# Convolution module of a hybrid decoder step: tap seeds in PSUM, thirds of a tile in strict order, sums of squares of two norms added up by TensorE

## The chip, the cores and the metric

The kernel runs on one core of one Trainium2 chip. The metric is the device time of one execution in microseconds, the median of the runs taken.

## The reference

One step of a two-layer decoder with D = 1024, for a prompt of 1024 tokens behind 16 meta tokens and for 8 sequences with 4 new tokens each. Layer 0 is a Conformer convolution module and a ConvFFN; layer 1 is attention over a latent paged cache and another ConvFFN. Everything is float32. The change touches the convolution module alone:

```python
def conv_module(x, prefix, w_pw1, b_pw1, w_dw, b_dw, ln_g, ln_b, w_pw2, b_pw2):
    a, g = jnp.split(x @ w_pw1 + b_pw1, 2, axis=-1)       # x is rms_norm(h): 1024 -> 2 x 1024
    u = a * jax.nn.sigmoid(g)
    y, tail = causal_dwconv(u, prefix, w_dw)              # 31 taps for each channel
    y = jax.nn.silu(layer_norm(y + b_dw, ln_g, ln_b))
    return y @ w_pw2 + b_pw2, tail                        # 1024 -> 1024

def key_nope(c, w_uk, knorm_nope):                        # c: a page of the cached latent, 128 x 128
    return rms_norm(jnp.einsum('btc,chd->bthd', c, w_uk), knorm_nope)
```

`key_nope` of the cache is needed late, in layer 1; its sums of squares depend on the cache alone, so the kernel uses that product as a filler from the start on.

## The kernel before

Activations lie transposed: 8 tiles of 128 channels (KD = 8) by T0 = 1074 columns of tokens, with NB = 9 blocks of 128 tokens. A float32 product is made of three passes (`xh`, `xl`: high and low part of the data; `wh`, `wl`: of the weights). A **filler** (`cache_norms`) is one group of work on the cache: three matmuls of 512 columns (L603) and the sum of squares of 8 heads of 64, in one of three ways: 8 ACT squares with an accumulator (L615); one ACT square (L606) and a DVE reduction (L611); or the square, two halvings on POOL (L610) and a short DVE reduction. `on_dve` and `on_pool` say which of the eight groups of a page set goes which way, and `HALVE` where POOL stops. There are 256 groups. `self.help` sends the splits of the cache pages (`cl`) to POOL instead of DVE.

The module runs in these stages:

- **First norm** (from L347). For each of 8 tiles ACT squares it (L275, L278) and DVE adds the square to a sum (L279); nine ones-matmuls (L287, 18 records of one pass each) turn the sum into one number per token, DVE makes 1/sqrt of it in 11 small operations (`rsqrt`, L251 to L256), and `spread` brings it to all partitions: a copy on DVE (L264), transposes (L266), a copy on ACT (L268). Then the tiles are scaled (L354) and split (L135 ACT, L136 DVE). 30 fillers are put into this stage (`FIRST`).
- **Tile 0** of the first product (`gemms`, 144 matmuls of 358 columns, L171), without fillers of its own.
- **Tiles 1 to 7** of the first product: a tile is cut into three thirds of 358 columns, each with a value and a gate half (48 matmuls, L395), a filler after every 6 matmuls. Behind a third come the sigmoid (L378, ACT) and the product u (L379, DVE). Each half has two PSUM banks. The scheduler, which sees the whole program, may let thirds overlap.
- **conv31**, for each tile, beside the next tile's product: DVE does 46 multiply-adds of 512 columns (L488): 16 taps for even, 15 for odd positions (`p0`, `p1`) and 16 for a combined sequence `s` = u odd + u even shifted (L477, `p2`). The running sum (`a0`, `a1`) lies in PSUM. The first term of each comes from ACT (L481) and is written to SBUF, into `fa` or `fb`. POOL makes the products for the last columns (L484) and for the 8 sequences (L502), which DVE reduces (L486, L504).
- **layer_norm**: the mean by TensorE (L529, 3 matmuls for each of 8 tiles, fillers between them: `FILL1` 2, `FILL0` 11), centering (L537, DVE), squares (L543, ACT), their sum on DVE and POOL (L549, L546, L551), then ones-matmuls, rsqrt and spread as above, with 15 fillers (`FILL2`) and 4 more behind (`NLN`).
- **pw2**: scaling (L426), SiLU (L428), split, and the second product (L171), with a filler after every 9 matmuls as long as there are any.

`high_priority` raises an operation for the scheduler; `manual_schedule` fixes TensorE's order as written, and `follow` adds an order without a wait.

Of the kernel before, what the change touches and what calls it, by code (L numbers as in the profile page):

```python
# [25 lines left out]
NB = 9  # L26
# [9 lines left out]
FILL0 = 11  # L36
FILL1 = 2
FILL2 = 15
NLN = 4
ONDVE0 = ()  # L40
ONDVE = (0,)
ONLN = (0, 4)
# [76 lines left out]
class Prog:  # L119
# [139 lines left out]
    def spread(self, r9, out, tn, ps=None):  # L259
# [3 lines left out]
        for c in range(3):  # L263
            nc.vector.tensor_copy(rx[:, 3 * c:3 * c + 3], r9[:, 3 * c:3 * c + 3].rearrange("p (a b) -> p a b", b=1).broadcast_to([128, 3, 128]))  # L264
            for b in range(3):
                nc.tensor.transpose(ps[:, c, b * 128:(b + 1) * 128], rx[:, 3 * c + b, :], self.cst("ident"))  # L266
            w = min(384, tn - 384 * c)
            nc.scalar.activation(out[:, 384 * c:384 * c + w], ps[:, c, :w], AF.Copy)  # L268

    def sq_add(self, sq, x, k, tn):  # L270
        nc = self.nc
        if k == 0:
            if sq.shape[1] > T0:
                nc.gpsimd.memset(sq[:, tn:], 0.0)
            nc.scalar.activation(sq[:, :tn], x, AF.Square)  # L275
            return
# [14 lines left out]
    def rows_rstd(self, sq, tn):  # L291
        r9, ps = self.token_rstd(self.sp, [sq[:, 128 * b:128 * (b + 1)] for b in range(NB)])
# [28 lines left out]
    def conv_phase(self):  # L321
# [3 lines left out]
        with ExitStack() as es:  # L325
# [40 lines left out]
            for c in range(KD):  # L366
                self.help = 0 < c < KD - 1
# [19 lines left out]
                else:  # L387
                    ch, cnt = T0 // 3, 0
                    for t in range(3):
                        ps = [p.tile([128, 1, 512], F32, name="g")[:, :, :ch] for p in (ga, gg)]  # L390
                        with self.manual():
                            for w, p in zip(ws, ps):
                                for k in range(KD):
                                    for i, (x, m) in enumerate(((w[0], xh), (w[0], xl), (w[1], xh))):
                                        nc.tensor.matmul(p[:, 0], x[:, k * 128:(k + 1) * 128], m[k][:, t * ch:t * ch + ch],  # L395
                                                         start=k == 0 and i == 0, stop=k == KD - 1 and i == 2)
# [3 lines left out]
                        glu(*ps, t)  # L400
                with self.manual():
# [30 lines left out]
            self.on_dve, self.on_pool = ONLN, ONPL1  # L432
# [3 lines left out]
            sq = self.rp.tile([128, T0], F32, name="sq")  # L436
            ahead = [self.weight(a["pw2"][ot], 1024) for ot in range(2)]
# [32 lines left out]
    def conv31(self, c, u, us, y, w31, wsum, pr):  # L470
# [6 lines left out]
        nc.vector.tensor_tensor(out=s, in0=u[:, 1, 0:535], in1=u[:, 0, 1:536], op=ALU.add)  # L477
        def taps(p, x, w, n, name):
# [5 lines left out]
            nc.gpsimd.tensor_tensor(out=r, in0=bass.AP(v.tensor, v.offset, [list(v.ap[0]), [1, m - ND], [1, n]]),  # L484
                                    in1=w.rearrange("p (c j) -> p c j", c=1).broadcast_to([128, m - ND, n]), op=ALU.mult)
# [16 lines left out]
        nc.gpsimd.tensor_tensor(out=p, in0=win, in1=w31[:, c:c + 1].broadcast_to([128, NS, 31]), op=ALU.mult)  # L502
# [16 lines left out]
    def layer_norm(self, ys):  # L519
# [4 lines left out]
        self.on_dve = ONLN0  # L524
        self.on_pool = ONPL0
# [5 lines left out]
        self.on_dve = ONLN  # L531
        self.on_pool = ONPL1
        sq = self.tp.tile([128, 1152], F32, name="sq", tag="c")
        odd = None
        with self.tc.high_priority(PRIO):
            for k in range(KD):
                nc.vector.scalar_tensor_tensor(out=v3(ys[k]), in0=mu[:, :, :ch], scalar=-1.0 / D, in1=v3(ys[k]), op0=ALU.mult, op1=ALU.add)  # L537
            for k in range(KD):
                if k == 0:
                    self.sq_add(sq, ys[k], 0, T0)  # L540
                    continue
                q = self.xpool(k).tile([128, self.tw], F32R, name=f"xl{k}").bitcast(F32)
                nc.scalar.activation(q, ys[k], AF.Square)  # L543
                if k in ONPOOL:
                    if odd is not None:
                        nc.gpsimd.tensor_tensor(out=odd, in0=q, in1=odd, op=ALU.add)  # L546
                    odd = q if odd is None else odd
                else:
                    nc.vector.tensor_tensor(out=sq[:, :T0], in0=sq[:, :T0], in1=q, op=ALU.add)  # L549
                if k == ADDAT:  # L550
                    nc.vector.tensor_tensor(out=sq[:, :T0], in0=sq[:, :T0], in1=odd, op=ALU.add)  # L551
# [15 lines left out]
    def cache_open(self, es):  # L567
# [12 lines left out]
        self.fill = self.cache_norms()  # L580
        self.on_pool = ()

    def cache_norms(self):
# [10 lines left out]
        for g in range(32):  # L594
            ch, cl = nxt
            for j in range(4):
                p = 4 * g + j
                for c in range(2):
# [1238 lines left out]
```

## Time and profile before

| | us |
|---|---|
| median of 3 runs (lowest to highest) | 2837.03 (2835.17 to 2849.47) |
| the profiled execution | 2836.05 |
| its span in the profile | 2834.3 |

| engine | busy us | share of the span |
|---|---|---|
| TensorE (PE) | 2675.1 | 94% |
| VectorE (DVE) | 1911.5 | 67% |
| ScalarE (ACT) | 1380.9 | 49% |
| GpSimd (POOL) | 665.5 | 23% |

The mean granted TensorE clock was 0.966 of full speed. Times in the rows below are microseconds from the start of the span. TensorE's matmuls are pipelined: the distance between two starts is what one costs, its own duration is longer.

### The profile page before, as it was taken

What the parts mean: (1) busy time and instruction counts of PE and PEld (TensorE: products, weight loads), DVE (VectorE), ACT (ScalarE), POOL (GpSimd) and SP (SyncE); (2) the same over time, 40 slices, a digit from 0 to 9 for tenths busy, and PEclk for the clock granted to TensorE, in tenths of its full rate; (3) what the DMA queues carried; (4) which work ended last, traced back from release to release, by engine and by line L of the source; (5) the groups of instructions that cost most, each with busy time, mean ns of one, the idle gap of its engine ahead of it and who ended that gap; (6) DMA issues with size and microseconds to landing.
All of it is one profiled execution on the core that took longest, in us unless ns stands there. A gap on an engine that the chain in (4) does not pass through costs nothing.

```text
span 2834.3 us, 47489 instructions
## 1 busy us (share of the span) xinstructions
PE 2675.1 (94%) x16916; PEld 2456.8 (87%) x16916; DVE 1911.5 (67%) x3521; ACT 1380.9 (49%) x4074; POOL 665.5 (23%) x923
## 2 busy tenths in 40 slices
PE   7999986999999999999799999988999999999999
PEld 5888864999999999999667676656999999999999
DVE  8899997569888874234776767565358777766131
ACT  6778778435554553023555564555335544544010
POOL 1457542005333330001201212100005333321000
PEclk9999997999999999999889999978999999999999
DMA  4111110412322236122100001257502222227122
GB/s 136 55 39 57 40 48 20 153 47 76 101 80 91 85 115 225 40 93 90 37 10 26 23 16 42 73 168 225 183 33 76 72 86 78 79 86 257 45 85 74
DMA packets 127778, 238.30 MB, mean 84 GB/s; under 512 B 39779, under 2 KB 81141, under 8 KB 127413
## 3 DMA queue, kind: packets, MB, share of 16 engines
q1 hardware_dynamic: 103828, 200.82, 22.1%
q0 software_dynamic: 9600, 32.36, 3.1%
q10 hardware_dynamic: 14112, 2.09, 0.4%
q8 instruction: 133, 2.18, 0.3%
q14 instruction: 105, 0.85, 0.1%
HBM read 183.90 MB, written 51.31 MB: 83 GB/s over the span
## 4 chain that ended last, share of the span: by engine, by line
PE 80%; DVE 7%; ACT 6%; DMA 2%; issue 2%; SPq 2%; POOL 0%; ACTq 0%; DVEq 0%
PE ps L742 29%; PE ps L171 22%; PE v L1280 5%; PE pk L603 4%; PE ps L791 3%; PE g L395 3%; PE p L147 2%; DVE a L488 2%; PE ps L193 2%; ACT qq L615 2%; PE ps L960 1%; PE p L1290 1%; PE s L1250 1%; PE p L1292 1%; PE p L1293 1%
## 5 line engine op out<-in xcount | busy, mean ns | idle before, releaser
L135 ACT ACTIVATE wh<-raw 128x512 fp32r<-128x512 f32 (+2 forms) x256 | 191.3, 750 | 566.3 <-PE ps L171 360.0
L136 DVE TENSOR_TENSOR wl<-raw,wh 128x512 fp32r<-128x512 f32 (+2 forms) x244 | 201.1, 828 | 104.9 <-ACT wh L135 102.8
L888 DVE TENSOR_TENSOR x<-ps,x 128x1074 f32<-128x1074 f32 (+1 forms) x48 | 60.9, 1270 | 289.5 <-PE ps L171 289.4
L712 DVE SCALAR_TENSOR_TENSOR c<-ub,c,c 128x1040 f32<-128x1040 f32 (+1 forms) x176 | 225.2, 1312 | 30.1 <-ACT c L709 29.3
L615 ACT ACTIVATE qq<-pk 128x64 f32<-128x64 f32 x936 | 198.2, 248 | 76.8 <-PE pk L603 76.2
L615 ACT ACTIVATION_READ_ACCUMULATOR qq<-pk 128x1 f32 x936 | 194.3, 232 | 0.1
L1280 PE MATMUL v<-pf,vf 128*128 128x512 f32 (+4 forms) x448 | 180.2, 486 | 11.8 <-ACT pf L1297 11.5
L707 POOL COPY sb<-ub 128x32 f32<-128x32 f32 x88 | 88.4, 1006 | 398.1 <-DVE ub L753 359.6
L610 POOL TENSOR_TENSOR sq<-sq 128x256 f32<-128x256 f32 x198 | 130.1, 659 | 181.7 <-ACT sq L606 174.4
L603 PE MATMUL pk<-ukh,ch 128*128 128x512 f32 x256 | 115.2, 451 | 47.2 <-ACT qq L615 17.1
L1297 ACT ACTIVATE pf<-p 128x512 f32<-128x512 f32 (+4 forms) x224 | 99.5, 450 | 122.9 <-DVE p L1295 102.2
L171 PE MATMUL ps<-xh,wh 128*128 128x358 f32 (+1 forms) x672 | 147.8, 328 | 2.6 <-DVE x L888 1.6
L171 PE MATMUL ps<-xh,wl 128*128 128x358 f32 (+1 forms) x672 | 147.3, 327 | 0.4 <-DVE wl L136 0.4
L171 PE MATMUL ps<-al,wh 128*128 128x358 f32 (+1 forms) x672 | 147.2, 327 | 0.0
L171 PE MATMUL ps<-xl,wh 128*128 128x358 f32 (+1 forms) x672 | 146.8, 326 | 0.0
L171 PE MATMUL ps<-ah,wl 128*128 128x358 f32 (+1 forms) x672 | 146.5, 326 | 0.0
L171 PE MATMUL ps<-ah,wh 128*128 128x358 f32 (+1 forms) x672 | 146.2, 326 | 0.0
L488 DVE SCALAR_TENSOR_TENSOR a<-u,c,a 128x512 f32<-128x512 f32 x200 | 137.8, 742 | 0.0
L709 ACT ACTIVATE c<-ub,c 128x1074 f32<-128x1074 f32 (+1 forms) x88 | 101.3, 1185 | 67.3 <-DVE ub L753 53.1
L395 PE MATMUL g<-xh,wh 128*128 128x358 f32 x336 | 111.1, 331 | 18.0 <-DVE u L379 16.2
L171 PEld LDWEIGHTS ps<-xh,wh 128*128 128x128 f32 x672 | 116.2, 190 | 4.8 <-ACT ah L135 2.2
L135 ACT ACTIVATE wh<-s 128x512 fp32r<-128x512 f32 x120 | 75.5, 630 | 87.8 <-PE ps L742 81.2
(585 smaller groups left out, 9116.2 us busy)
## 6 DMA issues: line engine op xcount, KB each, us to landing
raw<-wup SPq DMA_DIRECT2D x88, 512.0 KB, 3.5
pg<-ctn SPq DMA_DIRECT2D x128, 192.0 KB, 2.6
raw<-wdn SPq DMA_DIRECT2D x32, 448.0 KB, 3.4
raw<-pw SPq DMA_DIRECT2D x24, 512.0 KB, 3.7
d_a<-c POOLq DMA_DIRECT2D x22, 537.0 KB, 3.5
raw<-d_a SPq DMA_DIRECT2D x22, 537.0 KB, 4.9
d_a<-c POOLq DMA_DIRECT2D x22, 531.0 KB, 3.1
raw<-d_a SPq DMA_DIRECT2D x22, 531.0 KB, 5.5
```

Source lines behind the costliest of these rows:

```text
L135: return (nc.scalar.activation(h, src, AF.Copy), (eng or nc.vector).tensor_tensor(out=l, in0=src, in1=h.bitcast(F32), op=ALU.subtract))
L136: (eng or nc.vector).tensor_tensor(out=l, in0=src, in1=h.bitcast(F32), op=ALU.subtract))
L171: nc.tensor.matmul(p[:, c, :ch], s[:, k * 128:(k + 1) * 128], m[k][:, off + c * ch:off + (c + 1) * ch], start=k == 0 and i == 0, stop=k == ...
L395: nc.tensor.matmul(p[:, 0], x[:, k * 128:(k + 1) * 128], m[k][:, t * ch:t * ch + ch], start=k == 0 and i == 0, stop=k == KD - 1 and i == 2)
L488: nc.vector.scalar_tensor_tensor(out=p[:, :ND] if j == n - 1 else acc, in0=x[:, j:j + ND], scalar=w[:, j:j + 1], in1=p[:, :ND] if j == 1 e ...
L603: nc.tensor.matmul(ps, s[:, j, :], m[:, 512 * c:512 * c + 512], start=i == 0, stop=i == 2)
L610: nc.gpsimd.tensor_tensor(out=v[:, :, :n], in0=v[:, :, :n], in1=v[:, :, n:2 * n], op=ALU.add)
L615: nc.scalar.activation(q, ps[:, 64 * h:64 * h + 64], AF.Square, accum_out=ss[:, p, 8 * c + h:8 * c + h + 1])
L709: x = nc.scalar.activation(c, ub, AF.Copy, scale=wd[:, t, 2:3])
L712: nc.vector.scalar_tensor_tensor(out=c[:, 2:pe], in0=ub[:, tap:tap + pe - 2], scalar=wd[:, t, tap:tap + 1], in1=c[:, 2:pe], op0=ALU.mult, ...
L742: nc.tensor.matmul(ps, w[:, s], m[:, lo:hi], start=first and k == 0 and i == 0, stop=k == KD // 2 - 1 and i == 2, skip_group_check=True)
L1280: nc.tensor.matmul(o[:, at_:], vf[:m, b, c], p[:m, :512 - at_], start=b == 0, stop=last)
```

## The change

- **Tap seeds.** The first terms of `p0` and `p1` are written by ACT into the PSUM accumulator itself (`seed`), so the first tap reads PSUM and no longer SBUF; `p2` keeps its seed in SBUF. `p1` comes ahead of `p0`. POOL's products in conv31 wait for the add of `s` (`after`).
- **Thirds.** A third's first matmul follows the last matmul of the third before (`wedge`).
- **Norms.** Each of the eight squares goes to TensorE by itself: nine ones-matmuls for each (`add_rows`), added up in PSUM. In the first norm the blocks of tiles 4 to 7 come after fillers 2, 3, 4 and 6 (`SUMAT`). The adds on DVE and POOL go.
- **Fillers.** FILL0 13, FILL2 4, NLN 0; in the mean and the layer norm POOL halves down to one number (`halve` = 1), for 4 of 8 and for all groups, and no DVE reduction is left there. `help` holds in tile 7 too.

```diff
-FILL0 = 11
+FILL0 = 13
-FILL2 = 15
-NLN = 4
+FILL2 = 4
+NLN = 0
-ONPL0 = ()
-ONPL1 = (0, 3, 6)
+ONPL0 = (1, 3, 5, 7)
+ONPL1 = range(8)
+SUMAT = (0, 0, 0, 0, 2, 3, 4, 6)
...
+    def add_rows(self, t, q, k, n, tn, early=()):
+        with self.manual():
+            for b in range(NB):
+                lo = min(128 * b, tn - 128)
+                x = self.nc.tensor.matmul(t[:, 2 * b:2 * b + 2], q[:, lo:lo + 128], self.ones[:, 0:2], start=k == 0 and b == 0,
+                                          stop=k == n - 1 and b == NB - 1, skip_group_check=True)
+                self.follow(x, early)
+                early = ()
...
-                sq = self.tp.tile([128, 1152], F32, name="sq", tag="c")
                 for k in range(KD):
-                    self.sq_add(sq, xs[k], k, T0)
-                rstd = self.rows_rstd(sq, T0)
+                    q = self.tp.tile([128, 1152], F32, name="q", tag="c")
+                    nc.scalar.activation(q[:, :T0], xs[k], AF.Square)
+                    self.add_rows(t, q, k, KD, T0, self.pks[SUMAT[k] - 1:SUMAT[k]] if SUMAT[k] else ())
+                rstd = self.rows_rstd(t, ps, T0)
...
-                self.help = 0 < c < KD - 1
+                self.help = c > 0
...
+                                        self.follow(y, self.wedge)
+                                        self.wedge = []
...
+                        self.wedge = [y]
                         glu(*ps, t)
...
-        nc.vector.tensor_tensor(out=s, in0=u[:, 1, 0:535], in1=u[:, 0, 1:536], op=ALU.add)
+        first = nc.vector.tensor_tensor(out=s, in0=u[:, 1, 0:535], in1=u[:, 0, 1:536], op=ALU.add)
...
-            nc.scalar.activation(p[:, :ND], x[:, 0:ND], AF.Copy, scale=w[:, 0:1])
+            to = acc if seed else p[:, :ND]
+            nc.scalar.activation(to, x[:, 0:ND], AF.Copy, scale=w[:, 0:1])
...
-                                               in1=p[:, :ND] if j == 1 else acc, op0=ALU.mult, op1=ALU.add)
+                                               in1=to if j == 1 else acc, op0=ALU.mult, op1=ALU.add)
...
             for k in range(KD):
-                if k == 0:
-                    self.sq_add(sq, ys[k], 0, T0)
-                    continue
                 q = self.xpool(k).tile([128, self.tw], F32R, name=f"xl{k}").bitcast(F32)
                 nc.scalar.activation(q, ys[k], AF.Square)
...
+                self.add_rows(t, q, k, KD, T0)
```

TensorE's order in the first norm, before: `pk` is a filler, `ps<-ones` a block of nine ones-matmuls, `sq` the sum of the squares.

```order
L603 MATMUL pk_282<-ukh_127,cl_188 128x512
L603 MATMUL pk_282<-ukl_128,ch_187 128x512
L603 MATMUL pk_291<-ukh_127,ch_187 128x512
L603 MATMUL pk_291<-ukh_127,cl_188 128x512
L603 MATMUL pk_291<-ukl_128,ch_187 128x512
L287 MATMUL ps_449<-ones_59,sq_425 128x2 x9
L603 MATMUL pk_298<-ukh_127,ch_187 128x512
```

Of the change, the first rows of TensorE's program:

```order
L296 MATMUL ps_425<-ones_59,q_426 128x2 x9
L296 MATMUL ps_425<-ones_59,q_440 128x2 x9
L296 MATMUL ps_425<-ones_59,q_454 128x2 x9
L296 MATMUL ps_425<-ones_59,q_468 128x2 x9
L610 MATMUL pk_191<-ukh_127,ch_187 128x512
L610 MATMUL pk_191<-ukh_127,cl_188 128x512
L610 MATMUL pk_191<-ukl_128,ch_187 128x512
...
L296 MATMUL ps_425<-ones_59,q_482 128x2 x9
L610 MATMUL pk_259<-ukh_127,ch_187 128x512
```

Before, the seventh filler is followed by the only block; now four blocks stand at the program's start and the other four behind fillers 2, 3, 4 and 6. In all 23 fillers came ahead of that matmul, now 18.

DVE's order at a tile's start, before: L379 is the last glu of the new tile, L488 the taps, of which the first two read `fa`.

```order
L379 SCALAR_TENSOR_TENSOR u_2715<-g_3155,c1_58,sg_2716 128x179x2
L488 SCALAR_TENSOR_TENSOR fb_2633<-fb_2633,wsum_531,a0_2674 128x512
L498 TENSOR_TENSOR x2_2631<-fb_2633,fa_2632 128x520
L409 MEMSET u_2715 128x1
L477 TENSOR_TENSOR fb_3387<-u_2715 128x535
L486 TENSOR_REDUCE fa_3386<-ra1_3397 128x8
L488 SCALAR_TENSOR_TENSOR a0_3389<-u_2715,c1_58,fa_3386 128x512
L488 SCALAR_TENSOR_TENSOR a1_3395<-u_2715,c1_58,fa_3386 128x512
```

Of the change:

```order
L507 SCALAR_TENSOR_TENSOR fb_2713<-fb_2713,wsum_611,a1_2754 128x512
L517 TENSOR_TENSOR x2_2711<-fb_2713,fa_2712 128x520
L621 TENSOR_REDUCE ss_134<-sq_3420 128x8
L393 SCALAR_TENSOR_TENSOR u_2795<-g_3235,c1_58,sg_2796 128x179x2
L427 MEMSET u_2795 128x1
L495 TENSOR_TENSOR fb_3467<-u_2795 128x535
L507 SCALAR_TENSOR_TENSOR a1_3469<-u_2795,c1_58,a1_3469 128x512
L507 SCALAR_TENSOR_TENSOR a0_3475<-u_2795,c1_58,a0_3475 128x512
L505 TENSOR_REDUCE fa_3466<-ra1_3471 128x8
```

The last glu (L379, now L393) went behind the last tap of the tile before; the first taps (L488, now L507) read the accumulators and stand ahead of the reduction that waits for POOL.

TensorE's order around the second norm, before: L529 is the mean's last block; eight fillers stand before the ones-matmuls and as many behind them.

```order
L529 MATMUL ps_6484<-x7_6401,ones_59 128x358 x3
...
L603 MATMUL pk_7303<-ukh_127,ch_7048 128x512
L603 MATMUL pk_7303<-ukh_127,cl_7049 128x512
L603 MATMUL pk_7303<-ukl_128,ch_7048 128x512
L287 MATMUL ps_7417<-ones_59,sq_7116 128x2 x9
L603 MATMUL pk_7310<-ukh_127,ch_7048 128x512
```

Of the change:

```order
L610 MATMUL pk_7345<-ukl_128,ch_7048 128x512
L296 MATMUL ps_7140<-ones_59,xl0_7149 128x2 x9
L296 MATMUL ps_7140<-ones_59,xl1_7163 128x2 x9
...
L296 MATMUL ps_7140<-ones_59,xl7_7247 128x2 x9
L267 MATMUL ps_7140<-c1_58,rx_7373 128x128 x9
L172 MATMUL ps_7453<-xh0_7390,wh_7441 128x358 x3
L172 MATMUL ps_7453<-xl0_7391,wh_7441 128x358 x3
L172 MATMUL ps_7453<-xh0_7390,wl_7442 128x358 x3
L610 MATMUL pk_7464<-ukh_127,ch_7048 128x512
```

Four fillers stand ahead of the eight blocks, none between them, the transposes (L267) and pw2's first matmuls (L172); 13 fillers come inside pw2 instead of 3.

## Rows read from the trace of the kernel before

**Rows 1.** The page: the span, and the granted clock of TensorE, in tenths of full speed, in 40 equal slices of the span.

```profile
span 2834.3 us, 47489 instructions
...
PEclk9999997999999999999889999978999999999999
```

**Rows 2.** Timeline of TensorE in the first norm. Columns: start us, duration us, engine, line, operation and tiles, number, idle time before and what ended it.

```profile
21.52 0.63 PE L603 MATMUL pk<-ukh,ch 128*128 128x512 f32 x1
21.94 0.63 PE L603 MATMUL pk<-ukh,cl 128*128 128x512 f32 x1
...
26.44 2.06 PE L287 MATMUL ps<-ones,sq 128*128 128x2 f32 x18
28.36 0.48 PE L603 MATMUL pk<-ukh,ch 128*128 128x512 f32 x1
28.68 0.40 PE L603 MATMUL pk<-ukh,cl 128*128 128x512 f32 x1
28.91 0.39 PE L603 MATMUL pk<-ukl,ch 128*128 128x512 f32 x1
...
48.40 0.49 PE L171 MATMUL ps<-xl,wh 128*128 128x358 f32 x2
```

**Rows 3.** Timeline of ACT in the first norm, first and last square. Columns as before.

```profile
7.75 1.10 ACT L275 ACTIVATE sq<-x 128x1074 f32<-128x1074 f32 x1 [0.29 <-DMA x<-x]
...
22.25 1.09 ACT L278 ACTIVATE q<-x 128x1074 f32<-128x1074 f32 x1
```

**Rows 4.** Timeline of DVE in the first norm. Columns as before.

```profile
28.54 0.17 DVE L251 TENSOR_SCALAR nr_v<-ps 128x9 f32<-128x9 f32 x1 [0.20 <-PE ps L287]
...
32.63 1.47 DVE L264 COPY rx<-r 128x384 f32<-128x384 f32 x3
...
46.58 1.26 DVE L136 TENSOR_TENSOR xl<-x,xh 128x1074 fp32r<-128x1074 f32 x1
```

**Rows 5.** Busy time by stretch of the span. Columns: stretch, its length, busy us (and instructions) of TensorE, its weight loads, DVE, ACT and POOL, granted clock, DMA share, GB/s.

```profile
226.00:270.50 44.50, 41.31 (x218) 37.03 (x217) 43.01 (x71) 34.00 (x217) 28.92 (x34) 1.00 0.17 48
...
452.00:495.00 43.00, 27.43 (x85) 16.99 (x85) 29.53 (x40) 33.29 (x185) 15.42 (x14) 0.70 0.08 26
...
500.00:571.00 71.00, 70.54 (x425) 69.71 (x425) 32.45 (x30) 26.95 (x58) 2.83 (x7) 1.00 0.44 153
```

**Rows 6.** Timeline of DVE in the tiles, at the starts of three of them and in the last one; the last line is the summary of L488's first taps (number, shortest, median and longest in ns, first and last start).

```profile
135.35 0.06 DVE L409 MEMSET u<- 128x1 f32 x1 [1.32 <-ACT us L408]
135.44 0.83 DVE L477 TENSOR_TENSOR fb<-u 128x535 f32<-128x535 f32 x1
...
226.09 0.84 DVE L477 TENSOR_TENSOR fb<-u 128x535 f32<-128x535 f32 x1
...
227.03 4.40 DVE L488 SCALAR_TENSOR_TENSOR a<-u,c,fa 128x512 f32<-128x512 f32 x2
231.35 2.06 DVE L488 SCALAR_TENSOR_TENSOR a<-u,c,a 128x512 f32<-128x512 f32 x3
...
253.98 0.90 DVE L379 SCALAR_TENSOR_TENSOR u<-g,c,sg 128x358 f32<-128x358 f32 x1 [0.86 <-ACT sg L378]
...
359.93 0.84 DVE L477 TENSOR_TENSOR fb<-u 128x535 f32<-128x535 f32 x1
...
405.36 2.69 DVE L477 TENSOR_TENSOR fb<-u 128x535 f32<-128x535 f32 x1
...
430.92 0.69 DVE L136 TENSOR_TENSOR cl<-ct,ch 128x512 fp32r<-128x512 f32 x1 [2.56 <-ACT ch L135]
...
445.19 0.69 DVE L136 TENSOR_TENSOR cl<-ct,ch 128x512 fp32r<-128x512 f32 x1 [1.56 <-ACT ch L135]
...
451.32 0.70 DVE L498 TENSOR_TENSOR x<-fb,fa 128x520 f32<-128x520 f32 x1
...
L488 DVE SCALAR_TENSOR_TENSOR a<-u,c,fa x16: 746/1046/3519, 91.2 to 413.8; 128x512 f32<-128x512 f32 x16
```

**Rows 7.** Timeline of POOL at the start of the tile of 226.09.

```profile
227.48 3.40 POOL L502 TENSOR_TENSOR p<-us,c 128x992 f32<-128x992 f32 x1
```

**Rows 8.** TensorE's waits between 83 and 405 us: line, what it waited for, us in total, times, the longest.

```profile
PE g L395 <- DVE u L379: 16.2, 6, 3.0
```

**Rows 9.** Timeline around the second norm, TensorE, then DVE.

```profile
476.26 4.00 PE L287 MATMUL ps<-ones,sq 128*128 128x2 f32 x18 [2.23 <-DVE sq L551]
480.12 0.77 PE L603 MATMUL pk<-ukh,ch 128*128 128x512 f32 x1
...
494.97 1.26 PE L171 MATMUL ps<-xh,wh 128*128 128x358 f32 x3 [0.84 <-ACT xh L135]
...
455.25 9.56 DVE L537 SCALAR_TENSOR_TENSOR x<-ps,x 128x1074 f32<-128x1074 f32 x8 [3.23 <-PE ps L529]
...
480.30 0.17 DVE L251 TENSOR_SCALAR nr_v<-ps 128x9 f32<-128x9 f32 x1 [3.31 <-PE ps L287]
...
482.55 1.47 DVE L264 COPY rx<-r 128x384 f32<-128x384 f32 x3
```

**Rows 10.** Busy time by stretch, as in the fifth group, in three short stretches with ones-matmuls or right behind them.

```profile
476.30:480.10 3.80, 3.80 (x18) 3.80 (x19) 0.69 (x2) 0.00 (x0) 0.00 (x0) 0.50 0.00 0
...
589.60:592.10 2.50, 2.24 (x22) 2.16 (x20) 0.21 (x2) 0.00 (x0) 0.00 (x0) 1.00 0.04 7
592.20:595.50 3.30, 3.30 (x12) 3.30 (x13) 1.31 (x9) 0.00 (x0) 0.00 (x0) 0.50 0.00 0
```

More of the change, by code (lines that the diff above doesn't have):

```diff
@@ L143, in follow, with after @@
             self.tc.add_manual_dep(late.ins, x.ins.name, why, reason="order")
+    def after(self, late, early):
+        why = mybir.DependencyInfo(mybir.DependencyClass.Sync, mybir.DependencyReason.DATA)
+        self.tc.add_manual_dep(late.ins, early.ins.name, why, reason="order")
     def mm3(self, out, sh, sl, mh, ml, start=True, stop=True):
@@ L289, in token_rstd, with rows_rstd @@
         return r9, ps
-    def rows_rstd(self, sq, tn):
-        r9, ps = self.token_rstd(self.sp, [sq[:, 128 * b:128 * (b + 1)] for b in range(NB)])
+    def add_rows(self, t, q, k, n, tn, early=()):
[6 more added lines that the diff above has]
+                early = ()
+    def rows_rstd(self, t, ps, tn):
+        r9 = self.sp.tile([128, NB], F32, name="r9")
+        self.rsqrt(self.sp, r9, [(ALL, t[:, 0:2 * NB:2], 1.0 / D)], [128, NB])
         rstd = self.rp.tile([128, T0], F32, name="rstd")
@@ L394, in conv_phase @@
                                     for i, (x, m) in enumerate(((w[0], xh), (w[0], xl), (w[1], xh))):
-                                        nc.tensor.matmul(p[:, 0], x[:, k * 128:(k + 1) * 128], m[k][:, t * ch:t * ch + ch],
-                                                         start=k == 0 and i == 0, stop=k == KD - 1 and i == 2)
+                                        y = nc.tensor.matmul(p[:, 0], x[:, k * 128:(k + 1) * 128], m[k][:, t * ch:t * ch + ch],
+                                                             start=k == 0 and i == 0, stop=k == KD - 1 and i == 2)
+                                        self.follow(y, self.wedge)
+                                        self.wedge = []
                                         cnt += 1
@@ L431, in conv_phase @@
                 ll.append(l)
-            self.on_dve, self.on_pool = ONLN, ONPL1
             self.groups(NLN)
@@ L501, in conv31 @@
         win = bass.AP(v.tensor, v.offset, [list(v.ap[0]), [1, NS], [8, 31]])
-        nc.gpsimd.tensor_tensor(out=p, in0=win, in1=w31[:, c:c + 1].broadcast_to([128, NS, 31]), op=ALU.mult)
+        self.after(nc.gpsimd.tensor_tensor(out=p, in0=win, in1=w31[:, c:c + 1].broadcast_to([128, NS, 31]), op=ALU.mult), first)
         t = self.sp.tile([128, NS], F32, name="s")
@@ L530, in layer_norm @@
                 self.groups(FILL1 if k < KD - 2 else FILL0 if k < KD - 1 else 0)
-        self.on_dve = ONLN
         self.on_pool = ONPL1
-        sq = self.tp.tile([128, 1152], F32, name="sq", tag="c")
-        odd = None
+        sums = self.pp.tile([128, 3, 512], F32, name="ps")
+        t = sums[:, 2, 400:400 + 2 * NB]
         with self.tc.high_priority(PRIO):
@@ L538, in layer_norm @@
             for k in range(KD):
-                if k == 0:
-                    self.sq_add(sq, ys[k], 0, T0)
-                    continue
                 q = self.xpool(k).tile([128, self.tw], F32R, name=f"xl{k}").bitcast(F32)
                 nc.scalar.activation(q, ys[k], AF.Square)
[L544 to L551, printed above, removed]
+                self.add_rows(t, q, k, KD, T0)
         self.groups(FILL2)
         with self.tc.high_priority(PRIO):
-            return self.rows_rstd(sq, T0)
+            return self.rows_rstd(t, sums, T0)
     def pages(self, pt, slot, moves):
@@ L579, in cache_open @@
         self.ss = k1.tile([128, 128, H], F32, name="ss")
-        self.fill = self.cache_norms()
+        self.fill, self.pks, self.halve = self.cache_norms(), [], HALVE
         self.on_pool = ()
@@ L602, in cache_norms @@
                     for i, (s, m) in enumerate(((ch, self.ukh), (cl, self.ukh), (ch, self.ukl))):
-                        nc.tensor.matmul(ps, s[:, j, :], m[:, 512 * c:512 * c + 512], start=i == 0, stop=i == 2)
+                        x = nc.tensor.matmul(ps, s[:, j, :], m[:, 512 * c:512 * c + 512], start=i == 0, stop=i == 2)
+                    self.pks.append(x)
                     if 2 * j + c in self.on_dve or 2 * j + c in self.on_pool:
```

35 lines of the change are left out of this document (18 added, 17 removed).

## The prediction

> **What bounds the kernel now.** I read the page first: in the stretch that the change touches, TensorE's clock row dips once, in the seventh slice, 425 to 496 us [rows 1]. The order of instructions is the same before and after from the pw2 product on, so only the first 571 us can change. I went through them by stage, with the windows view, and inside each stage with the timeline of the engine that ends last there.
>
> Three stages count. In the **first norm** TensorE works off fillers at 0.43 us a matmul until about 25 us, then at 0.23; the reader is to see the same kind of row at two paces [rows 2]. The norm itself is a chain of ACT squares, DVE adds, one block of ones-matmuls at 26.44, the rsqrt on DVE, the transposes and the first split; the regular run of matmuls starts at 48.40 [rows 2 to 4]. In the **tiles** both TensorE (41.31) and DVE (43.01) fill a period of 44.5 [rows 5]. DVE is the later one: five periods from 135.44 to 359.93 make 44.9 each [rows 6], and it loses time at the tile's start, where two first taps take 4.40 us while three later ones take 2.06 [rows 6]; POOL's product of 3.40 us runs beside the slow one [rows 7]. TensorE waits for DVE's glu 16.2 us in all, six times, up to 3.0 [rows 8]. In the **layer norm** the chain is mean, eight centerings, squares and adds, ones-matmuls, rsqrt, rstd, SiLU, split, first pw2 matmul at 494.97, 42.95 us after DVE's last tap operation ends at 452.02 [rows 6, 9]. There the clock is granted at 0.70 on average [rows 5].
>
> **First norm.** Seven DVE adds and one block of 18 records go; eight blocks of 18 records come, four of them ahead of the first filler, the others between the fillers. At 2.4 GHz a block takes 1.92 us (26.44 to 28.36) [rows 2], at 1.2 GHz 3.86 (476.26 to 480.12) [rows 9]. Which of the two holds decides this term. What the rows show: at 476.3 to 480.1 TensorE was busy with ones-matmuls all 3.80 us and the granted clock was 0.50; at 589.6 to 592.1 twenty ones-matmuls of a later norm ran at 1.00, and the clock was 0.50 behind them, from 592.2 to 595.5, though TensorE was busy all along [rows 10]. So a busy row of ones-matmuls neither raised the clock nor held it. The first fillers ran at the low pace as well [rows 2]. I take the low level for the whole start.
> The first square ends at 8.85 and the last at 23.34 [rows 3], so TensorE sets the pace: 8 blocks x 3.86 = 30.9, and six filler groups between them at 3 x 0.43 = 1.28, 7.7 us: the last block ends at about 47.4 instead of 28.4. Four more filler groups at the low pace (5.1) lie beside the rsqrt, which took 4.1 from 28.54 with other work in between [rows 4] and 2.25 without (480.30 to 482.55) [rows 9]. From the end of the ones block to the regular run it was 20.0 us before; with fewer fillers between the transposes, and DVE freed of the pending sums, I take 15.8: rsqrt and first spread 2.8, transposes with four filler groups about 7, first product and split 2.4, and the next product, two reductions and xl 3.6 (xl alone 1.26 [rows 4]). The run starts at about 63.2: **+14.8**. The lower end is -2 (blocks at 1.92, the last one behind the last square, at 25 to 26), the upper +17 (some 2 us more from fillers that wait for their banks). Five filler groups fewer stand ahead of the tiles; they come again early in tile 1, and cost nothing as long as DVE's taps on tile 0 end later than TensorE; at the end of that tile, at 135.35, DVE waited 1.32, for ACT's copies [rows 6].
> The Trainium skill (TensorE: Matmul & The Clock Gate, section What's actually happening) has it that activity of TensorE releases the throttle. Taken at its word, with ones-matmuls as activity, the blocks would run at the full clock; that is the first rival below. The stretches at 476 and 592 speak against it [rows 10].
>
> **Tiles.** The seed goes into PSUM, and POOL's products wait for the add of s. A first tap then reads one SBUF tensor and one PSUM tensor, as every later tap does, and those ran at 0.69 beside POOL's work (231.35, three in 2.06) [rows 6]: 4.40 becomes 1.38, so 3.0 less for each of tiles 1 to 6. The glu wait of 0.86 (253.98) goes with the strict order of the thirds, since each third's pair is then complete sooner; in exchange the tile's last glu stands directly ahead of the add of s, which needs ACT's copies of u: some 0.6 of waiting, half of the 1.32 seen at 135.35 [rows 6]. DVE then needs 44.9 - 3.0 - 0.9 + 0.6 = 41.6, TensorE 41.3: I take 42.0, which is -2.9 for each of six periods, -17.4. In the last tile POOL now helps (three splits of cl, 0.69 each, leave DVE, and with them the waits for ACT of 2.56 and 1.56), and the add of s takes 0.84 instead of 2.69 [rows 6]: 1.9 + 2.0 + 4.1 = -8.0. Sum **-25.4**. The bounds: at least the last tile and 0.5 for each period, -11; at most DVE without any wait, 41.0, -31. POOL's new halvings in the mean and the layer norm lie beside TensorE.
> The Trainium skill (SBUF — State Buffer, section Who interferes with whom) says that a DVE instruction with two SBUF inputs and a GpSimd instruction that reads SBUF shut each other out for the whole instruction, and that one with a single SBUF input does not. The trace agrees: the longest first tap took 3.52 us [rows 6], POOL's product 3.40. By this page the add of s, with two SBUF inputs, could still collide with POOL's halvings of fillers.
>
> **Layer norm and pw2.** Five DVE adds and two POOL adds go; the squares go straight to TensorE, which runs eight blocks in a row behind the last mean and four filler groups, from about 6.3 us after the last tap (first centering 3.2 and 1.2 [rows 9], its square 1.1 [rows 3], some waiting for ACT). The clock is full then and falls in their course, as it did at 592 [rows 10]; I let a third of them run at the full level: 2.7 blocks at 1.92 and 5.3 at 3.86 end 32.0 us after the last tap, against 28.1 before. From there to the first pw2 matmul I take 9.4 instead of 14.85 (480.12 to 494.97) [rows 9]: eight filler groups lay there, 8 x 0.70 = 5.6 at the full clock, and none does now. 32.0 + 9.4 against 42.95: -1.6. But of the fillers that lay there ten are left for the pw2 run, which TensorE fills (70.54 of 71) [rows 5], at 3 x 0.23 = 0.70: +7. **+5.4**; with the blocks all at the full clock (8 x 1.92 = 15.4) -4.9, all at the low one (30.9) +10.6.
>
> **Sum:** 14.8 - 25.4 + 5.4 = -5.2 on the profiled execution's 2836.05, which lies 0.98 below the median of the runs: **2831**.
>
> **Rivals.** *Ones-matmuls keep the clock up.* Start -2, tiles -25.4, layer norm -4.9: 2804. For it: the blocks are dense, and the fillers between them may raise the clock early. Against it: the clock that stayed low and fell with TensorE busy [rows 10].
> *TensorE's strict order makes the last third late.* With nothing of the next third ahead of time, the last third's sigmoid and glu, which DVE needs for the add of s, come after DVE has finished its taps; TensorE has no slack to make it up (41.3 of 42). It decides from 2.4 us of DVE waiting at each tile's start: then the six periods gain 0.5 each, 14.4 of the tile term are lost, and the time is 2845, slower than before; with the layer norm's blocks all at the low clock, 2850. For it: TensorE already waits up to 3.0 at a tile's start [rows 8]. Against it: the fillers are spread evenly between the pieces, and the two banks for each half leave one third of lead.
> *The change doesn't do what it says:* the first taps still stand still while POOL's product runs, because it is started right behind the add of s, at the same moment. 6 x 3.0 are lost: 2849. Against it: the later taps' 0.69 beside POOL.
>
> **How the numbers follow.** About 0.5% (14.2 us) is what a measurement of this kernel can tell from no change: faster is below 2822.8, slower above 2851.2. The forecast has 0.60, with its own range of 2817 to 2845 (tiles -18 to -31, start +10 to +17, layer norm 0 to +10, not all at one end); the full clock 0.18; the late third 0.10; the stalled taps 0.10; 0.02 is left. Faster: all of the second and a quarter of the first, 0.34. Slower: the upper end of the last two, 0.08. No change: 0.58. The range from 2804 to 2849 leaves out half of the full-clock case and parts of the two slow ones.
>
> **What would show it.** Right: ones-blocks 3.9 us apart in the first 45 us, regular run at about 63; first taps at 0.7, DVE's add of s 42 us apart; the layer norm's blocks falling from 1.9 to 3.9; pw2 longer by 7. Wrong: blocks of 1.9 from the start (then about 2804); adds of s 44 us or more apart, with DVE waiting for the glu or with first taps of 3.4; the first pw2 matmul well under 38 us after the last tap.

## The result and the profile after

The change took 2849.63 us (median of 20 runs, 2846.11 to 2856.06) against 2843.01 for the kernel before, run beside it (20 runs, 2835.17 to 2850.19): ratio 1.0025, 95% interval 1.0016 to 1.0034. Slower by 0.25%, where 2831 was forecast. That forecast stood on three runs of the kernel before with a median of 2837.03; as a difference it was -5.2 us, against +6.6 between the medians here. The profiled execution took 2846.30 (before: 2836.05), its span 2844.5.

Where the time lies, from the starts of the same operations in both traces (us):

| stage | before | change | difference | forecast |
|---|---|---|---|---|
| regular run of matmuls starts | 48.40 | 59.90 | +11.5 | +14.8 |
| tile 0 (from add of s to add of s) | 47.51 | 51.80 | +4.3 | 0 |
| tiles 1 to 6 | 269.92 | 267.07 | -2.9 | -17.4 |
| last tile, to its last operation | 46.66 | 35.05 | -11.6 | -8.0 |
| from there to pw2's first matmul | 42.95 | 48.96 | +6.0 | -1.6 |
| pw2, to its 384th matmul | 68.41 | 74.97 | +6.6 | +7 |
| behind pw2, to the end | 2270.9 | 2267.2 | -3.7 | 0 |
| the span | 2834.3 | 2844.5 | +10.2 | -5.2 |

TensorE in the first norm, the row that answers to [rows 2] (columns as there):

```profile
7.96 15.52 PE L296 MATMUL ps<-ones,q 128*128 128x2 f32 x72 [7.96 <-ACT q L362]
23.34 0.77 PE L610 MATMUL pk<-ukh,ch 128*128 128x512 f32 x1
...
26.05 3.83 PE L296 MATMUL ps<-ones,q 128*128 128x2 f32 x18
...
36.29 3.83 PE L296 MATMUL ps<-ones,q 128*128 128x2 f32 x18
...
42.69 2.25 PE L296 MATMUL ps<-ones,q 128*128 128x2 f32 x18
44.80 0.48 PE L610 MATMUL pk<-ukh,ch 128*128 128x512 f32 x1
```

Four blocks take 15.52, the next three 3.83 each: by this pace the low level (1.2 GHz; a block took 3.86 at a granted clock of 0.50 in [rows 9, 10]), with TensorE never idle. The level is read from the pace, because the view prints a granted clock of 1.00 for this stretch: the trace has no entry of the clock before its first rise, near 43 us. Only the last block, during which the pace changes, is faster.

One tile's start in the change, DVE, then ACT, then TensorE; it answers to [rows 6, 7]. The first line of each is still of the tile before: DVE's last operation, the sigmoid of TensorE's last third, and the last matmul of that third.

```profile
279.23 0.70 DVE L517 TENSOR_TENSOR x<-fb,fa 128x520 f32<-128x520 f32 x1
281.10 0.29 DVE L621 TENSOR_REDUCE ss<-sq 128x8 f32<-128x128 f32 x1 [1.17 <-POOL sq L619]
281.32 0.88 DVE L393 SCALAR_TENSOR_TENSOR u<-g,c,sg 128x358 f32<-128x358 f32 x1
282.93 0.06 DVE L427 MEMSET u<- 128x1 f32 x1 [0.72 <-ACT us L426]
283.02 0.98 DVE L495 TENSOR_TENSOR fb<-u 128x535 f32<-128x535 f32 x1
283.92 1.40 DVE L507 SCALAR_TENSOR_TENSOR a<-u,c,a 128x512 f32<-128x512 f32 x2
```

```profile
280.75 0.54 ACT L392 ACTIVATE sg<-g,c 128x358 f32<-128x358 f32 x1
...
282.61 0.25 ACT L426 ACTIVATE us<-u 128x32 f32<-128x32 f32 x1
282.74 1.32 ACT L500 ACTIVATE a<-u,c 128x512 f32<-128x512 f32 x2
...
284.36 0.62 ACT L614 ACTIVATE sq<-pk 128x512 f32<-128x512 f32 x1
```

```profile
279.58 0.33 PE L409 MATMUL g<-xh,wl 128*128 128x358 f32 x1
...
282.93 0.33 PE L409 MATMUL g<-xh,wl 128*128 128x358 f32 x1
285.03 0.50 PE L610 MATMUL pk<-ukh,ch 128*128 128x512 f32 x1 [1.77 <-ACT sq L614]
285.37 0.57 PE L610 MATMUL pk<-ukh,cl 128*128 128x512 f32 x1
285.74 0.63 PE L610 MATMUL pk<-ukl,ch 128*128 128x512 f32 x1
```

The first taps are fast, 1.40 for two. But DVE has no tap left to do when TensorE's last third ends (279.91; DVE's last operation ends at 279.93); the glu, the copies of u, the seeds and a filler's square follow each other on DVE and ACT, and TensorE stands 1.77 us for that square. Behind this stop its clock falls. Six tiles have such a stop, and the clock falls in three of them; two of these take 44.9 us where the tiles like them take 43.4 (columns as in [rows 5]; the third number from the end of a line is the granted clock, 0.50 from 285.4). The last two lines belong to the second norm, below:

```profile
283.30:285.00 1.70, 0.00 (x0) 0.00 (x0) 1.70 (x3) 1.70 (x8) 1.05 (x4) 1.00 0.54 103
285.40:288.70 3.30, 3.30 (x11) 3.02 (x10) 3.30 (x7) 2.46 (x18) 3.30 (x3) 0.50 0.35 139
462.60:465.90 3.30, 3.28 (x30) 3.28 (x30) 3.30 (x4) 3.30 (x5) 3.30 (x8) 1.00 0.03 7
466.00:490.00 24.00, 24.00 (x116) 24.00 (x115) 2.78 (x3) 4.45 (x5) 3.63 (x17) 0.51 0.00 1
```

The waits of the tiles (who waits for whom, us in total, times, longest), of DVE and TensorE; the glu wait of [rows 8] is gone:

```profile
DVE ss L621 <- POOL sq L619: 17.4, 25, 2.4
```

```profile
PE pk L610 <- ACT sq L614: 12.9, 10, 1.8
```

The second norm, TensorE, for [rows 9]; the last two lines of the stretches above are its blocks:

```profile
457.21 1.97 PE L547 MATMUL ps<-x,ones 128*128 128x358 f32 x6
...
462.62 27.53 PE L296 MATMUL ps<-ones,xl 128*128 128x2 f32 x144
493.05 0.90 PE L267 MATMUL ps<-c,rx 128*128 128x128 f32 x3 [2.90 <-DVE rx L265]
494.54 0.90 PE L267 MATMUL ps<-c,rx 128*128 128x128 f32 x3 [0.58 <-ACT rstd L269]
496.02 0.90 PE L267 MATMUL ps<-c,rx 128*128 128x128 f32 x3 [0.58 <-ACT rstd L269]
502.30 1.26 PE L172 MATMUL ps<-xh,wh 128*128 128x358 f32 x3 [5.38 <-ACT xh L132]
```

The last tap ends at 453.34; the mean's last block comes 3.9 us later (1.2 before), the blocks are at full speed for 3.3 us and at the low level for 24, and behind them TensorE, with no filler to run, waits 9.4 us in four pieces for DVE and ACT.

### The profile page after: what moved, and what is told of

Its sections match the earlier page's. It is cut to its first block, busy times and chain, and to the rows that moved or that the text cites. A ratio compares the mean times of both kernels' runs of the same rounds, so it can differ in the third digit from the quotient of the medians.

```text
span 2844.5 us, 47733 instructions
## 1 busy us (share of the span) xinstructions
PE 2711.8 (95%) x17168; PEld 2503.8 (88%) x17168; DVE 1871.2 (66%) x3506; ACT 1362.0 (48%) x3776; POOL 682.5 (24%) x1007
## 4 chain that ended last, share of the span: by engine, by line
PE 85%; DVE 5%; ACT 4%; issue 2%; DMA 2%; SPq 1%; POOL 0%; ACTq 0%; DVEq 0%
PE ps L752 29%; PE ps L172 22%; PE pk L610 6%; PE g L409 5%; PE v L1290 5%; PE ps L801 3%; PE ps L296 2%; PE p L148 2%; PE ps L194 2%; PE ps L970 1%; PE p L1300 1%; PE p L1302 1%; PE p L1303 1%; PE s L1260 1%; ACT qq L625 1%
## 5 line engine op out<-in xcount | busy, mean ns | idle before, releaser
L625 ACT ACTIVATE qq<-pk 128x64 f32<-128x64 f32 x776 | 164.7, 242 | 71.3 <-PE pk L610 70.9
L619 POOL TENSOR_TENSOR sq<-sq 128x128 f32<-128x128 f32 (+3 forms) x264 | 151.2, 579 | 151.7 <-ACT sq L614 141.8
L625 ACT ACTIVATION_READ_ACCUMULATOR qq<-pk 128x1 f32 x776 | 160.5, 226 | 0.0
L172 PE MATMUL ps<-xh,wh 128*128 128x358 f32 (+1 forms) x672 | 147.6, 328 | 7.6 <-ACT xh L132 5.4
L507 DVE SCALAR_TENSOR_TENSOR a<-u,c,a 128x512 f32<-128x512 f32 x216 | 150.6, 745 | 0.0
L172 PE MATMUL ps<-xh,wl 128*128 128x358 f32 (+1 forms) x672 | 147.4, 327 | 0.0
L172 PE MATMUL ps<-al,wh 128*128 128x358 f32 (+1 forms) x672 | 147.2, 327 | 0.0
L172 PE MATMUL ps<-xl,wh 128*128 128x358 f32 (+1 forms) x672 | 146.9, 326 | 0.0
L172 PE MATMUL ps<-ah,wl 128*128 128x358 f32 (+1 forms) x672 | 146.5, 326 | 0.0
L172 PE MATMUL ps<-ah,wh 128*128 128x358 f32 (+1 forms) x672 | 146.2, 326 | 0.0
L172 PEld LDWEIGHTS ps<-xh,wh 128*128 128x128 f32 x672 | 116.4, 190 | 10.8 <-ACT xh L132 6.2
L172 PEld LDWEIGHTS ps<-xl,wh 128*128 128x128 f32 x672 | 116.3, 189 | 1.2 <-DVE xl L133 0.5
```

The costliest lines, as they stand in the source:

```text
L172: nc.tensor.matmul(p[:, c, :ch], s[:, k * 128:(k + 1) * 128], m[k][:, off + c * ch:off + (c + 1) * ch], start=k == 0 and i == 0, stop=k == ...
L619: nc.gpsimd.tensor_tensor(out=to, in0=v[:, :, :n], in1=v[:, :, n:2 * n], op=ALU.add)
L625: nc.scalar.activation(q, ps[:, 64 * h:64 * h + 64], AF.Square, accum_out=ss[:, p, 8 * c + h:8 * c + h + 1])
```

## The experiments

One quantity runs through them: the **lead**, the end of DVE's last operation of a tile less the end of TensorE's last third for the next one. For each kernel: start of the regular run, tile 0's period, mean period of tiles 1 to 5, lead in them, last tap, from there to pw2, pw2 (us, one profile each); then the ratio to the kernel before with its interval.

| | run | tile 0 | period | lead | last tap | to pw2 | pw2 | ratio |
|---|---|---|---|---|---|---|---|---|
| before | 48.4 | 47.5 | 44.9 | 4.3 | 452.0 | 43.0 | 68.4 | |
| change | 59.9 | 51.8 | 44.1 | 0.0 | 453.3 | 49.0 | 75.0 | 1.0025 |
| e1 | 47.3 | 45.4 | 42.4 | 4.0 | 424.9 | 47.8 | 75.2 | 0.9937 (0.9921 to 0.9954) |
| e2 | 63.7 | 51.9 | 44.1 | 0.0 | 456.3 | 39.9 | 74.5 | 1.0010 (0.9998 to 1.0022) |
| e3 | 63.4 | 54.8 | 44.0 | 0.0 | 461.3 | 47.3 | 74.8 | 1.0046 (1.0029 to 1.0062) |
| e4 | 47.8 | 45.4 | 42.4 | 4.0 | 424.8 | 47.6 | 67.5 | 0.9918 (0.9897 to 0.9938) |
| e5 | 57.0 | 46.9 | 44.1 | 0.25 | 444.7 | 46.5 | 78.6 | 1.0013 (1.0003 to 1.0024) |
| e6 | 47.9 | 46.7 | 42.0 | 5.2 | 429.3 | 41.3 | 67.2 | 0.9882 (0.9856 to 0.9907) |
| e7 | 47.4 | 46.7 | 42.9 | 4.0 | 436.3 | 44.7 | 68.5 | 0.9922 (0.9903 to 0.9940) |
| e8 | 47.6 | 45.5 | 42.5 | 4.0 | 424.9 | 61.7 | 65.9 | 0.9937 (0.9914 to 0.9960) |
| e9 | 63.6 | 43.2 | 42.2 | 4.0 | 438.4 | 46.6 | 81.4 | 0.9984 (0.9973 to 0.9995) |
| e10 | 50.5 | 50.3 | 43.1 | 1.0 | 437.9 | 46.0 | 75.3 | 0.9951 (0.9933 to 0.9969) |
| e11 | 48.0 | 46.7 | 42.0 | 5.2 | 424.4 | 42.5 | 67.0 | 0.9874 (0.9849 to 0.9898) |
| e12 | 48.0 | 49.1 | 42.6 | 5.0 | 439.9 | 43.9 | 66.2 | 0.9936 (0.9916 to 0.9957) |

**e1.**

```diff
-                    self.add_rows(t, q, k, KD, T0, ...)
-                rstd = self.rows_rstd(t, ps, T0)
+                    self.sq_add(sq, xs[k], k, T0)
+                rstd = self.old_rstd(sq, T0)        # one block, as before
```

> The change, with the first norm's squares added up by DVE again and one block of ones-matmuls; all else as changed. Theory (the eight blocks at the low clock delay the start): the regular run of matmuls starts at 48 to 50 us instead of 59.9, every later stage starts 10 to 11.5 earlier, and the kernel is 10 us faster than the change. Rival (the start is caught up, since TensorE's fillers set the pace of tile 1): the run starts earlier but the add of s of tile 1 moves by less than 4 us.

The run starts at 47.3 and nothing is caught up; more than that, the tiles are 1.6 us shorter each and tile 0 6.4 shorter. The last tap is 28.5 earlier, for 12.6 at the start: the first norm's blocks cost more than twice their own delay. In the runs the kernel is some 25 us faster than the change (0.9937 against 1.0025), where 10 were expected.

**e2.** The layer norm's squares added on DVE and POOL again.

```diff
-                self.add_rows(t, q, k, KD, T0)
+                ...                                 # L543 to L551 of before
+            return self.old_rstd(sq, T0)
```

> The change, with the layer norm's squares added up by DVE and POOL again and one block; fillers as changed. Theory (eight blocks, most at the low clock, are on the path): first pw2 matmul some 41 to 43 us after the last tap instead of 49.0, 6 to 8 us faster than the change. Rival (the chain behind the blocks without fillers at the low clock is what costs): still 47 or more, within 2 us of the change.

From last tap to pw2 9.1 less: the blocks were the path. The start was 3.8 later than in the change by the same instructions there, since the matmuls kept the low pace longer (to 52.4 instead of 42.7); that hides part of the gain, which is some 4 us in the runs (1.0010 against 1.0025).

**e3.**

```diff
-            self.after(nc.gpsimd.tensor_tensor(...), first)
+            nc.gpsimd.tensor_tensor(...)
```

> The change without POOL's wait for the add of s. Theory (the wait holds POOL's queue, the halvings behind it come late, and DVE's reductions and TensorE's fillers wait for them): DVE's waits for POOL fall from 17.4 us to under 8, tile periods go from 43.4 to 44.9 down to about 42.5, some 6 to 8 us in all. Rival (the wait keeps the add of s apart from POOL's product): the add of s takes 2.6 us or more instead of 0.98, and the periods stay or grow by 1 to 2 us each.

The theory fell: DVE's waits for POOL stay at 16.4 and the periods at 44.0. The rival fell for most tiles too; the add of s collided with POOL in the first and last alone (2.22 and 3.24). What held POOL's halvings back was not POOL's wait.

**e4.** `conv31`, the strict order and `help` of the change put into the kernel before.

> The kernel before with the tile part of the change alone: seeds in PSUM, POOL's products behind the add of s, thirds in strict order, POOL's help in the last tile; both norms and all fillers as before. Theory (tiles gain, norms lose): last tap 12 to 14 us earlier than before, the layer norm's length within 3 us of before, the kernel 10 to 14 us faster than before. Rival (the gain of the last tile is eaten by fillers in the mean, which TensorE and ACT have not finished): the mean's last block starts 3 to 4 us after the last tap or later, and the kernel gains under 8.

At the last tap the tile part gains 27.2 us. That is near the 25.4 of the prediction and twice the 12 to 14 expected for this run, but the agreement of the sum is luck in part: tile 0 gives 2.1 (forecast 0), tiles 1 to 6 give 14.1 (17.4), the last tile 11.5 (8.0). As the rival said, the mean's fillers then end late (its last block starts 5.3 us behind the last tap), and 4.7 go in the layer norm; but the kernel gains some 23 us in the runs, not under 8.

**e5.**

```diff
-FIRST = 30
+FIRST = 25
```

> The change with FIRST 25 instead of 30: five fillers leave the head of tile 1 (six in a row there, as before, instead of eleven) and come in pw2 (18 instead of 13). The eight blocks of the first norm stay. Theory (eleven fillers in a row cost TensorE its lead over DVE, and the tiles then wait in a ring): tile 0's period 46 to 48 us instead of 51.8, the later periods 42.4 to 42.8 instead of 43.4 to 44.9, DVE's waits for POOL under 8 us, pw2 3.5 longer, 8 to 11 us faster than the change in all. Rival (the late start itself, not the fillers, sets the pace of the tiles): the periods stay at 43.4 or more, and the kernel is within 3 us of the change.

Tile 0 as the theory had it, the periods as the rival had it, with a lead of only 0.25. The six fillers in a row are those of e1, whose periods are 42.4.

**e6.** `conv31` of the change alone in the kernel before. **e7.** `wedge` alone.

> The kernel before with the seeds in PSUM and POOL's products behind the add of s alone; thirds, norms and fillers as before. Theory (the first taps' 3.0 us were DVE's, and DVE sets the period): first taps 0.7 each, periods 42.4 to 43.5 instead of 44.5 to 44.9, 8 to 12 us faster than before. Rival (TensorE and the overlapping thirds set the period): periods 44 or more, under 4 us faster.

> The kernel before with the strict order of the thirds alone. Theory (the order removes the glu waits, DVE still has the slow first taps): periods 44.0 to 44.6, 2 to 4 us faster than before. Rival (the order lets a third's end be late, TensorE loses its lead): periods 45 or more, slower than before.

Each alone gives most of the tiles' gain, 2.9 and 2.0 us a tile, and in the runs some 33 and 22 us, where 8 to 12 and 2 to 4 were expected. In e6's 42.0 TensorE is busy for 41.2 to 42.2; in e7's 42.9 DVE is busy for 42.5. Together (e4, 42.4) they give no more than the seeds, for then TensorE is the bound (busy for 41.9).

**e8.** As e1, with `FILL2 = 3` and:

```diff
                 self.add_rows(t, q, k, KD, T0)
+                if k < KD - 1:
+                    with self.manual():
+                        self.groups(2)
```

> As e1 (first norm as before), and in the layer norm two fillers between any two of the eight blocks of ones-matmuls, so that no fillers are left for pw2 but some three. Theory (the fillers hold the clock at the full level): the last block ends 30 to 34 us after the last tap, the first pw2 matmul comes at 40 to 44, pw2 takes 66, 13 to 17 us faster than e1. Rival (the ones-matmuls let the clock fall all the same): blocks and fillers at the low level, last block 50 us or more after the last tap, pw2's start at 62 or more, 5 us or more slower than e1.

The rival was right on the clock: in the order that came out ten fillers stand among the eight blocks (none between the third and the fourth) and three behind the last, and the clock fell in the second block and stayed low, TensorE being busy throughout. At the 384th matmul of pw2 the kernel is 4.7 us behind e1, where 5 or more were expected for the whole; the runs end even.

```profile
433.72 2.17 PE L298 MATMUL ps<-ones,xl 128*128 128x2 f32 x18
435.75 0.47 PE L628 MATMUL pk<-ukh,ch 128*128 128x512 f32 x1
...
436.52 3.38 PE L298 MATMUL ps<-ones,xl 128*128 128x2 f32 x18
439.76 0.77 PE L628 MATMUL pk<-ukh,ch 128*128 128x512 f32 x1
```

```profile
440.00:474.00 34.00, 34.00 (x134) 31.39 (x134) 0.00 (x0) 7.30 (x12) 18.80 (x59) 0.50 0.00 0
```

**e9.** The change with `FIRST = 20`. **e10.** e1 with `FIRST = 35`.

> The change with FIRST 20: one filler at the head of tile 1 instead of eleven, ten more left for pw2. The eight blocks of the first norm stay. Lead here means: DVE's last operation of a tile less the end of TensorE's last third of the next tile; it is 4.3 us before, 0.0 in the change, 0.25 with five fillers moved, 4.0 with the first norm as before. Theory (the lead decides whether the last glu is late, whether ACT then stands at its copies of u with the fillers' squares behind them, and whether TensorE waits for those squares): lead 3 us or more, periods 42.4 to 42.8, TensorE's waits for ACT's squares in the tiles under 5 us instead of 12.9. Rival (the late start changes the tiles by some other way): periods 43.9 or more again. Pw2 takes 7 us longer in either case.

> As e1 (first norm as before, regular run at 47.3), with FIRST 35: twelve fillers in a row at the head of tile 1 instead of six. Theory (the lead decides): tile 0's period 49 to 51 us instead of 45.4, the lead lost (under 0.5 us), periods 43.4 or more as in the change, 8 to 12 us slower than e1 less 3.5 in pw2. Rival (the late start decides): the periods stay at 42.4 and the kernel is within 4 us of e1.

e9 shows that the late start alone is not the cause: its start is at 63.6, later than in the change, and yet the lead is 4.0, the periods 42.2, and TensorE does not wait for ACT's squares in the tiles. Its tile start (DVE, then POOL) shows the glu done ahead of the last operation, and no wait:

```profile
228.26 0.88 DVE L393 SCALAR_TENSOR_TENSOR u<-g,c,sg 128x358 f32<-128x358 f32 x1
228.96 1.35 DVE L517 TENSOR_TENSOR x<-fb,fa 128x520 f32<-128x520 f32 x1
230.26 0.06 DVE L427 MEMSET u<- 128x1 f32 x1
```

```profile
227.34 2.42 POOL L133 TENSOR_TENSOR wl<-raw,wh 128x1024 fp32r<-128x1024 f32 x1
```

e10 is the reverse: a start only 3.1 later than in e1, twelve fillers in a row. Six more fillers (4.2 us of TensorE at 0.70) make tile 0 4.8 longer and each later period 0.6; that is less than the 1.0 or more that was expected, the lead is 1.0 and not under 0.5, and DVE waits again:

```profile
226.21 0.86 DVE L408 SCALAR_TENSOR_TENSOR u<-g,c,sg 128x358 f32<-128x358 f32 x1 [0.81 <-ACT sg L407]
227.53 0.06 DVE L442 MEMSET u<- 128x1 f32 x1 [0.46 <-ACT us L441]
```

So fillers early in tile 1 are not free. What carries their cost into the later tiles stays open, for three reasons:

- The lead on tile 0 does not order the kernels: it is 0.25 in e5 and -0.3 in e10, and yet e10 has the shorter periods afterwards (43.1 against 44.1); and e5 has the six fillers of e1.
- `FIRST` also shifts which of the eight groups of a page set, with its own way by ACT, DVE or POOL, falls at a tile's start; a tile holds 24 groups, so the shift stays the same in all tiles. It is 5 places in e5 and e10, 10 in e9, none between the change and e1. No run moves the number of fillers alone.
- The lead goes with the written order. In every kernel with 3.98 or more the last glu stands ahead of DVE's last operation, as in e9; in the change, e2, e3, e5 and e10 it stands behind it. In e1, e4, e7, e8 and e9 that operation, with two SBUF inputs, also runs beside POOL's split of the next weights, which starts 1 us behind the end of the third: in e9 it takes 1.35, not the 0.70 of the change, and ends 0.55 behind the split. By these rows the 3.98 that comes again in all five is the length of this chain and not a measure of slack.

**e11.** e6 with `help = c > 0` and, in the mean, POOL halving 4 of 8 groups down to one number.

> As e6 (the seeds alone), with POOL's help in the last tile and the mean's fillers halved on POOL for 4 of 8 groups, as in the change; both norms and the fillers' counts as before. Theory (what held the last tile were splits and waits for ACT, what held the mean were ACT's eight squares for a filler): last tile 36 us instead of 42.9, the mean's last block 3 us after the last tap instead of 4.2 to 7.3, 6 to 8 us faster than e6, the fastest of all. Rival (the gained time is waited for at the mean): under 3 us.

Last tile 38.3 instead of 42.9, but pw2 starts 1.2 later after it; 2.6 us in the profiles, within the intervals in the runs. The rival holds. It is the fastest median of all, 2803.19, 1.3% under the kernel before.

**e12.** e6 without POOL's wait.

> As e6 (the seeds alone) without POOL's wait for the add of s. Theory (the seed itself takes the 3.0 us away, since a tap that reads PSUM does not collide with POOL's product): first taps 0.7 each, periods within 0.7 of e6's. Rival (the wait matters as well): the add of s collides with POOL's product, 2.5 us or more in each tile, periods 1.5 us or more longer.

Both are at work, and the kernel is some 15 us slower than e6 in the runs (0.9936 against 0.9882). The first taps are fast without the wait, but the add of s, two SBUF inputs, then collides with POOL in four of eight tiles (number; shortest, median, longest in ns), first of e12, then of e6:

```profile
L481 DVE TENSOR_TENSOR fb<-u x8: 835/1914/3518, 87.6 to 395.5; 128x535 f32<-128x535 f32 x8
```

```profile
L481 DVE TENSOR_TENSOR fb<-u x8: 703/776/1099, 87.4 to 386.4; 128x535 f32<-128x535 f32 x8
```

## Why the prediction was wrong

- **The step that failed** is the sentence on the five fillers that leave the first norm, come again early in tile 1 "and cost nothing as long as DVE's taps on tile 0 end later than TensorE". The condition was taken as given, though the row named beside it, DVE waiting 1.32 at the end of that tile, speaks against it, and it did not hold: the lead on tile 0 was 1.4 us before, five fillers are 3.5, and in the change it was -2.0. Tile 0 grew by 4.3, and the lead never came back: with the faster taps TensorE is busy for 41.5 us of a tile and DVE for 40.0, so TensorE has nothing to catch up with. That the fillers cost is shown by e10 against e1 (six more) and e9 against the change (ten fewer: tile 0 8.6 shorter, the periods 1.8).
- **What it cost.** With a lead of 0 the tile's start becomes a ring (glu, copies, seeds, square, filler). Tiles 1 to 6 gained 2.9 instead of 17.4. Of the missing 14.5, 11.3 are the difference to e1, which has the same tile part and whose tiles run at 42.4; some 3 are missing there too. In the 11.3 are also the falls of the clock in three tiles, 1.5 each. That the link runs through ACT's order is read from the rows, not tried; the written order and the kinds of fillers are rivals that no run separates from the lead.
- **The late third** was among the rivals with 0.10, at the right place and with the right size (0.5 a period, 0.48 measured), but by the wrong cause, and the size is luck in part, since the falls of the clock are in it: TensorE was not late by the strict order (e7, e4: lead 4.0).
- **The tile term itself** was nearly right without the norms' part: -2.9 a tile forecast, -2.5 in e4, which has the whole tile part, and -2.9 in e6. The last tile gave 11.6 instead of 8.0.
- **The first norm** was right in its mechanism and 3.3 too dear (+11.5). The last block ended at 44.8 instead of 47.4, since TensorE began at 7.96 and not at 8.85 and the pace rose during that block (2.1 for it instead of 3.86); from there to the regular run it was 15.1 for 15.8. In e2, e3 and e9, with the same blocks, the run started at 63.4 to 63.7, as forecast (63.2), in e5 at 57.0: it depends on when the clock rises. The low pace lasts to 52.4 in e2 and e9; in e5 a block at 26.2 is already fast (2.15) and a later one slow again (3.83). What sets that time no run shows.
- **The layer norm** failed by 7.6 (+6.0 for -1.6). The mean's fillers were not done when the shorter last tile ended (2.7); the blocks ended 36.8 us after the last tap and not 32.0, since they began at 9.3 and not at 6.3, and the clock fell after 3.3 us; and the chain behind them took 12.2 instead of 9.4, of which TensorE waited 9.4 for DVE and ACT. I had taken the fillers out of 14.85 as if they were all of its waiting.
- **pw2** was right: 6.6 for 7. The full-clock rival fell (rows above, e8); that the first taps still stall fell too.
- 3.7 us come back behind pw2, where both programs are the same on every engine; the difference of the same operations moves between 8.5 and 15 there. What moves it was not tried.

## What to carry to other kernels

When two engines share a loop with little slack, ask which of them leads, by how much and what sets that lead, and what work moved ahead of the loop does to it: 3.5 us moved into the first pass, with a later start, came out as 16 over the loop (e1 against the change, beyond the start's delay). And sums that TensorE makes by ones-matmuls are dear where its clock is low or may fall; adds on an engine that waits anyway were cheaper in both norms.

## What the hardware showed beyond the forecast

TensorE was busy with ones-matmuls and fillers from 7.96 to 42.7 us without a gap, and kept the pace of 1.2 GHz (3.83 a block, 0.43 a matmul of a filler). In e8 the granted clock fell to 0.50 in the middle of busy work and stayed there for 34 us and more, though a third of that time were fillers. The Trainium skill (TensorE: Matmul & The Clock Gate, section What's actually happening) says that activity releases the throttle; here a row that the trace calls busy was not enough. A stop of 1.77 us at a tile's start was followed by 3.3 us at 1.2 GHz in three tiles of the change, and not in the three others with the same stop.

An operation of DVE with two SBUF inputs took longer beside POOL's work in two places: a tile's last operation 1.35 in e9 beside a split of 2.42, and 0.70 in the change without it; the add of s up to 3.52 in e12, and 0.70 to 1.1 in e6.
